# Memory attention with the query weights folded into the keys and the output weights into the values

## The chip, the cores and the metric

The kernel is one launch on one core of a Trainium2 chip. The core has a matrix engine (TensorE, "PE" in the profile, its weight loads "PEld"), a vector engine (VectorE, "DVE"), a scalar engine for activations (ScalarE, "ACT"), a general engine (GpSimd, "POOL") and a queue engine (SyncE, "SP"), which in this kernel issues all transfers. The metric is device time in microseconds of one execution; lower is better.

## The reference

One layer of an encoder, in fp32, for 2048 prompt tokens and 32 sample tokens (2080 columns), width 1024. Every sub-layer is `x + RMSNorm(sublayer(RMSNorm(x)))`:

1. token mixing: banded attention and gated linear attention from one input projection, joined by an output projection `w_o`;
2. attention with 4 heads of 256 into 256 memory tokens;
3. a SwiGLU feed-forward layer, hidden width 2816.

The change touches step 2 and its neighbours. Its core is

```
k = (m @ w_mk), v = (m @ w_mv)            # m = RMSNorm(mem), 256 x 1024, 4 heads of 256
q = h @ w_mq                              # h = RMSNorm(x)
p = softmax(q k^T / 16)                   # per head, over 256 memory tokens
out = concat_heads(p v) @ w_mo
```

The 32 sample tokens use keys and values from a cache instead of `k` and `v`. `k` and `v` of the prompt's memory are outputs too.

## The kernel before, in words

Activations lie feature-major: 128 features on the partitions, tokens along the free dimension. Nearly every fp32 product is made of three matmuls in a reduced-precision type (fp32r): each operand is split into a high part (a cast on ACT) and the remainder (a subtraction on DVE or POOL), and `mm3` (L485 in the profile) issues high x high, high x low, low x high into one PSUM bank. `mm3_steps` (L1329) is the same in pieces that can be interleaved with other work. `split` is L424/L425, `split_own` (in place) L429/L430. `load_w` and `w_piece` bring a weight tile of 128 x 512 from DRAM and split it.

The order of issue on each engine is not that of the program text. A class `Order` collects all operations, gives them costs and priorities, plans a schedule over all engines and then pins each engine to the planned order. So work of neighbouring stages is interleaved, and an engine never overtakes an instruction that it was given earlier. Where a pool of buffers closes and another opens over the same memory, the first users of the new tiles wait for the last users of the old.

The stages, in time: input projection and the two mixers, with the projections of the memory to keys and values (`mem_kv`) and the output projections of blocks 0 to 2 (`out_proj`, four blocks of 512, 512, 512, 544 tokens) interleaved, up to about 1250 us; the queries of the first 416 tokens (`mem_q0`, tile mqps at L1329) and the output projection of the last block (wops) up to about 1350; the memory stage up to about 1815; the feed-forward layer to the end.

The memory stage works on five blocks of 416 tokens (`CB`). `mem_q` projects the queries of the next block (mqps, L485; stored to DRAM, L1598); `mem_attn` loads them per head, makes scores (ms, sample tokens at L1635), softmax over rows of 104 or 128 tokens (L1637 to L1641), transposes (mpt, L1644) and the product with the values (mpv, sample tokens at L1654; mo, L1656/L1657). `mem_out` multiplies with `w_mo` (mops; copy to y at L1671). `mem_fin` applies the norm after the sub-layer, adds the residual and applies the norm ahead of the feed-forward layer (L1685 to L1690, `norm_fm` at L442 to L448), and stores x2d and h2d in DRAM in blocks of 416.

The feed-forward layer works on three blocks of two halves (`CF`: 348, 346, 346 tokens a half). Gate and up products (pg, pu) are computed by a scheme of seven instead of eight sub-products over the halves of tokens and features, the down product (pdn) accumulates into an SBUF tile acc (copy of the first product at L571, additions at L532). `finish` of a block makes the norm (n_ps L1876, rstd L434/L435), scales (L1883), adds the residual and stores `y_t` (L1886). Each block has new acc tiles, from a pool of two.

Of the kernel before, what the change touches and what calls it, by code (L numbers as in the profile page):

```python
# [393 lines left out]
def encoder_step(ctx, tc, ins, outs):  # L394
# [12 lines left out]
    QLEAD = 0.5  # L407
# [29 lines left out]

    def norm_fm(pool, pspool, xs, n, name, tag="dense", rbufs=2):
        acc = pool.tile([P, n], F32, tag="nacc", name=name + "_acc")
        for k in range(KT):  # L440
            if k == 0:
                ACT.activation(acc, xs[k], AF.Square)  # L442
            else:
                sq = pool.tile([P, n], F32, tag="nsq", name=f"{name}_sq{k}")
                ACT.activation(sq, xs[k], AF.Square)
                (POOL if k % 2 else DVE).tensor_tensor(out=acc, in0=acc, in1=sq, op=ALU.add)
        ps = pspool.tile([P, 512], F32, tag=tag, name=name + "_ps")
        PE.matmul(ps[:, :n], lhsT=ones, rhs=acc, start=True, stop=True)  # L448
        return rstd_of(pool, ps[:, :n], n, D, name + "_r", rbufs)

    def apply_split(pool, xs, g, r, n, dst, name):
        for k in range(KT):
            hf = pool.tile([P, n], F32, tag="hf", name=f"{name}_hf{k}")
            DVE.scalar_tensor_tensor(out=hf, in0=xs[k], scalar=g[:, k : k + 1], in1=r, op0=ALU.mult, op1=ALU.mult)
            hi, lo = dst[k]
            split(hi, lo, hf, POOL)
# [52 lines left out]
    mvd = dpool.tile([NMEM, D], F32, name="mvd")  # L509
    CB = [(i * 416, 416) for i in range(5)]  # L510
    h2d = [dpool.tile([D, n], F32, name=f"h2d{b}") for b, (_, n) in enumerate(CB)]
    x2d = [dpool.tile([D, n], F32, name=f"x2d{b}") for b, (_, n) in enumerate(CB)]
    qmd = [dpool.tile([D, n], F32, name=f"qmd{b}") for b, (_, n) in enumerate(CB)]
# [433 lines left out]
    with ExitStack() as ph:  # L947
# [448 lines left out]
        def mem_kv():  # L1396
            mv = []

            def first(tag):
                mv.clear()  # L1400
                for k2 in range(KT // 2):
                    m_ = mp.tile([P, 2, 544], F32R, tag="mov", name=f"mm{tag}_{k2}")
                    for j in range(2):
                        raw = sp.tile([P, 544], F32, tag="hr", name=f"mm{tag}_r{k2}_{j}")[:, :NMEM]
# [14 lines left out]
            def value(g4):  # L1419
                w = load_w(wp, ins["w_mv"][0], g4 * 256, 256, f"wmv{g4}")  # L1420
                for tt in range(2):
                    ps = pd.tile([P, 512], F32, tag="dense", name=f"mvps{g4}_{tt}")
                    yield from mm3_steps(ps[:, :256], [((mv[k][:, 0, tt * P : (tt + 1) * P], mv[k][:, 1, tt * P : (tt + 1) * P]), w[k]) for k in range(KT)], 12)
                    vf = sp.tile([P, 544], F32, tag="st", name=f"mvf{g4}_{tt}")[:, :256]
                    DVE.tensor_copy(vf, ps[:, :256])
                    SP.dma_start(mvd[tt * P : (tt + 1) * P, g4 * 256 : (g4 + 1) * 256], vf)
                    SP.dma_start(outs["mem_v"][0, 0].rearrange("t h d -> t (h d)")[tt * P : (tt + 1) * P, g4 * 256 : (g4 + 1) * 256], vf)
                    if tt == 0:
                        yield

            return [partial(first, 0)] + [partial(key, m) for m in range(KT)], [partial(first, 1)] + [partial(value, g) for g in range(4)]

        def mem_q0():
            n = CB[0][1]
            mv = {}

            def first():

                for k in range(KT):
                    pl, tag, w = [(lp, "ks", 768), (lp, "nb", 640), (gp, "W", 576), (xp, "xw", 544)][k // 2]  # L1440
                    kw = {"bufs": 2} if tag == "W" else {}
                    mv[k] = pl.tile([P, 2, w], F32R, tag=tag, name=f"hq0_{k}", **kw)
                    SP.dma_start(mv[k][:, 1, :n].bitcast(F32), h1d[0][k * P : (k + 1) * P, :n])
                    split_own(mv[k][:, :, :n], True)

            def query(m):
                w = load_w(wp, ins["w_mq"][0], m * P, P, f"wmq0_{m}")
                ps = (pd, pb, pb)[m % 3].tile([P, 512], F32, tag=("dense", "band", "band")[m % 3], name=f"mqps0_{m}")
                yield from mm3_steps(ps[:, :n], [(w[k], (mv[k][:, 0, :n], mv[k][:, 1, :n])) for k in range(KT)])
                qf = sp.tile([P, 544], F32, tag="hr", name=f"qf0_{m}")[:, :n]  # L1450
                ACT.mul(qf, ps[:, :n], 0.0625)
                SP.dma_start(qmd[0][m * P : (m + 1) * P, :], qf)

# [99 lines left out]
    with ExitStack() as ph:  # L1553
# [142 lines left out]
        for b in range(len(CB)):  # L1696
# [7 lines left out]
            if b != len(CB) - 2:  # L1704
                for it in proj:
                    it()
# [321 lines left out]
```

## Time and profile before

| | |
|---|---|
| median of 3 runs | 3280.02 us (3275.47 to 3282.64) |
| profiled execution: its span, the only time that is kept of it | 3277.0 us |
| instructions | 57899 |
| mean granted TensorE clock | 0.984 |
| busy: PE, DVE, ACT, POOL | 96%, 74%, 52%, 22% |
| transfers | 486.31 MB, mean 148 GB/s |

A span is the time from the first to the last instruction. Busy shares are averages over stages with different limits. In a view of groups, a line reads: code line, engine, operation, output<-inputs, partitions x elements, count | busy us, mean ns of one | idle time of the engine just before, with what ended it. In the chain (the work that ended last, followed back from the end) a row is start, length, engine, tile and count. In the waits a row is engine, tile and line, what it waited for, then total us, number of waits and the longest. Stretches are given in us from the span's start.

### The profile page before, as it was taken

How to read it: one execution, taken by the hardware profiler on the slowest of the kernel's cores; microseconds unless marked ns; L12 is line 12 of the kernel's file. 1: busy time of each engine (PE TensorE's matmuls, PEld its weight loads, DVE VectorE, ACT ScalarE, POOL GpSimd, SP SyncE). 2: the span in 40 equal slices, each digit the busy share in tenths (PEclk: the TensorE clock that was granted, in tenths of full speed). 3: DMA queues.
4: the chain of work that ended last, by engine and by line, in shares of the span. 5: the costliest groups of instructions: out<-in, count | busy, mean ns of one | idle time of the engine just before them, and what ended most of it. 6: DMA issues, size and time to landing. Idle time of an engine off the chain costs nothing.

```text
span 3277.0 us, 57899 instructions
## 1 busy us (share of the span) xinstructions
PE 3156.6 (96%) x21387; PEld 3022.0 (92%) x21387; DVE 2416.9 (74%) x4474; ACT 1719.9 (52%) x3706; POOL 717.1 (22%) x933
## 2 busy tenths in 40 slices
PE   7898999799999999999999899999899999899998
PEld 7888999698888888999999799999899999899998
DVE  7976976576575756777777877777977778977776
ACT  5645655656676666566665643334544334444344
POOL 0200100345474545410101111111211111311111
PEclk9999999899999999999999999999999999999999
DMA  5569273876585757765655522222432222422223
GB/s 150 178 168 297 101 222 120 262 227 193 177 269 152 239 169 229 221 191 179 204 175 179 166 91 71 76 78 78 136 111 78 76 73 63 130 79 77 78 78 96
DMA packets 490076, 486.31 MB, mean 148 GB/s; under 512 B 78528, under 2 KB 427881, under 8 KB 489793
## 3 DMA queue, kind: packets, MB, share of 16 engines
q1 hardware_dynamic: 489793, 482.61, 47.2%
q8 instruction: 168, 2.75, 0.3%
q14 instruction: 115, 0.94, 0.1%
HBM read 369.78 MB, written 113.83 MB: 148 GB/s over the span
## 4 chain that ended last, share of the span: by engine, by line
PE 88%; DVE 5%; DMA 3%; ACT 2%; issue 1%; SPq 1%; POOL 0%; DVEq 0%; ACTq 0%; POOLq 0%
PE pdn L485 15%; PE pg_X L485 8%; PE pu_X L485 7%; PE wops L1329 6%; PE mops L485 5%; PE mqps L485 4%; PE pg_Y L485 4%; PE pu_Y L485 4%; PE po L1063 4%; PE s L1058 2%; PE pg_Z L485 2%; PE pu_Z L485 2%; PE pt L1083 2%; PE ms L485 2%; PE g_s L1263 2%; PE wva_X L485 1%
## 5 line engine op out<-in xcount | busy, mean ns | idle before, releaser
L485 PE MATMUL pdn<-u,wd 128*128 128x346 f32 (+1 forms) x3168 | 520.2, 323 | 25.7 <-DVE acc L571 24.4
L485 PEld LDWEIGHTS pdn<-u,wd 128*128 128x128 f32 x3168 | 509.4, 190 | 27.7 <-DVE acc L571 25.3
L425 POOL TENSOR_TENSOR u<-sg,u 128x346 fp32r<-128x346 f32 (+1 forms) x132 | 165.4, 1264 | 1152.9 <-ACT u L424 611.7
L424 ACT CAST wg_s<-wg_r 128x512 fp32r<-128x512 f32 x231 | 139.1, 620 | 480.5 <-PE pdn L485 183.5
L532 DVE TENSOR_TENSOR acc<-acc,pdn 128x346 f32<-128x346 f32 (+1 forms) x464 | 235.8, 513 | 89.1 <-PE pdn L485 88.8
L485 PE MATMUL pg_X<-mf,wg_s 128*128 128x346 f32 (+1 forms) x1584 | 278.1, 324 | 6.6 <-ACT wg_s L424 5.3
L485 PE MATMUL pu_X<-mf,wu_s 128*128 128x346 f32 (+1 forms) x1584 | 275.2, 322 | 0.0
L485 PEld LDWEIGHTS pg_X<-mf,wg_s 128*128 128x128 f32 x1584 | 258.4, 190 | 8.2 <-ACT wg_s L424 5.7
L485 PEld LDWEIGHTS pu_X<-mf,wu_s 128*128 128x128 f32 x1584 | 256.9, 189 | 0.4
L1329 PE MATMUL wops<-om,wo_s 128*128 128x512 f32 (+1 forms) x960 | 214.4, 362 | 0.5 <-POOL om L430 0.5
L485 PE MATMUL mops<-mo,wmo_s 128*128 128x416 f32 x960 | 193.7, 353 | 2.1 <-DVE y L1671 1.2
L425 DVE TENSOR_TENSOR wu_s<-wu_r,wu_s 128x512 fp32r<-128x512 f32 x231 | 155.0, 696 | 39.1 <-ACT wu_s L424 39.0
L425 DVE TENSOR_TENSOR wd<-wd_r,wd 128x512 fp32r<-128x512 f32 x132 | 93.8, 715 | 121.7 <-ACT wd L424 121.6
L485 PEld LDWEIGHTS mops<-mo,wmo_s 128*128 128x128 f32 x960 | 177.1, 188 | 6.7 <-issue 1.9
L1329 PEld LDWEIGHTS wops<-om,wo_s 128*128 128x128 f32 x960 | 149.3, 188 | 20.5 <-issue 2.2
L485 PE MATMUL mqps<-m,wmq_s 128*128 128x416 f32 x768 | 163.6, 357 | 4.7 <-DVE m L430 4.2
L424 ACT CAST wu_s<-wu_r 128x512 fp32r<-128x512 f32 x231 | 136.6, 619 | 50.0 <-DVE wu_r L529 23.2
L425 DVE TENSOR_TENSOR wg_s<-wg_r,wg_s 128x512 fp32r<-128x512 f32 x231 | 158.7, 694 | 0.9 <-ACT wg_s L424 0.7
L1063 PE MATMUL po<-prt,v 128*128 128x128 f32 x1120 | 158.1, 281 | 1.2 <-PE mkps L1329 0.9
L1063 PEld LDWEIGHTS po<-prt,v 128*128 128x128 f32 x1120 | 145.3, 194 | 9.3 <-issue 2.9
L485 PE MATMUL pu_Y<-mf,wu_s 128*128 128x346 f32 (+1 forms) x792 | 140.1, 324 | 7.4 <-DVE up L532 5.7
L485 PEld LDWEIGHTS mqps<-m,wmq_s 128*128 128x128 f32 x768 | 139.8, 189 | 6.8 <-DVE m L430 4.4
(450 smaller groups left out, 7197.0 us busy)
## 6 DMA issues: line engine op xcount, KB each, us to landing
wg_r<-in_w_ffn_gate_dram SPq DMA_DIRECT2D x66, 512.0 KB, 4.4
wu_r<-in_w_ffn_up_dram SPq DMA_DIRECT2D x66, 512.0 KB, 3.5
wd_r<-in_w_ffn_down_dram SPq DMA_DIRECT2D x66, 512.0 KB, 3.4
wmq_r<-in_w_mq_dram SPq DMA_DIRECT2D x80, 256.0 KB, 3.0
wmo_r<-in_w_mo_dram SPq DMA_DIRECT2D x80, 256.0 KB, 3.0
q<-qd SPq DMA_DIRECT2D x32, 512.0 KB, 4.5
wo_r<-in_w_o_dram SPq DMA_DIRECT2D x64, 256.0 KB, 4.1
nb<-nbd SPq DMA_DIRECT2D x16, 640.0 KB, 7.6
```

What stands on the lines that cost most here:

```text
L424: ACT.copy(hi, src)
L425: (lo_eng or DVE).tensor_tensor(out=lo, in0=src, in1=hi.bitcast(F32), op=ALU.subtract)
L485: PE.matmul(ps, lhsT=a, rhs=b, start=first and i == 0, stop=last and i == len(seq) - 1, skip_group_check=skip)
L532: eng.tensor_tensor(out=out, in0=a, in1=b, op=ALU.add)
L1058: PE.matmul(ps_out, lhsT=q[:, 2 * i + e, q0 : q0 + nq], rhs=ks[:, e, k0 : k0 + ncol], start=i == 0, stop=i == 1)
L1063: PE.matmul(po[:, e * P : e * P + n], lhsT=v[:kk, j, e * 64 : e * 64 + P], rhs=prt[:kk, j, :n], start=j == 0, stop=j == len(rows) - 1)
L1083: PE.transpose(ptp[:kk, j, :n], pr[:n, c0 : c0 + kk], ident[:n, :n])
L1263: PE.matmul(sps[bk, li, :], lhsT=lh, rhs=rh, start=True, stop=True)
L1329: PE.matmul(ps, lhsT=a, rhs=b, start=i == 0, stop=i == len(seq) - 1)
```

## The change

The memory attention is computed in another association. Per head, `q k^T / 16 = h (Wq_h k_h^T / 16) = h G_h` with G_h of 1024 x 256, and `(p v_h) Wo_h = p (v_h Wo_h) = p H_h` with H_h of 256 x 1024.

- `mem_kv` projects the values transposed (as the keys) and normalises mem once; the values' output is transposed on the host.
- `mem_fold` takes the place of `mem_q0` ahead of the last output projection: it multiplies each head's keys with `w_mq` (handed over transposed by the host, `w_mq_t`) to gd[h], and its values with `w_mo` to hd[h], both in DRAM.
- The weight pool closes before the memory stage. That stage holds all four G in one tile gT, and works in 8 chunks of 256 tokens: scores of two heads at a time from h, 512 columns wide, softmax, transposes, and a store of the transposed probabilities to ptd. It no longer multiplies with values.
- The 32 sample tokens, whose keys and values are the cached ones, go the old way (queries, scores, values, output) in plain fp32, in pieces between the last chunks.
- The output product (probabilities with H) is made for the three feed-forward blocks in the buffers of the feed-forward stage (`mem_block`), with the norms and the residual per half block; x2d and h2d are stored by feed-forward block.
- In the feed-forward layer the two acc tiles are allocated once and serve all blocks, rstd stays in PSUM, `y_t` is stored in four pieces of two rows a half instead of two of four, and operand buffers are taken in another order.

The diff, cut to its core:

```diff
-    CB = [(i * 416, 416) for i in range(5)]
-    qmd = [dpool.tile([D, n], F32, name=f"qmd{b}") for b, (_, n) in enumerate(CB)]
+    mvd = dpool.tile([D, NMEM], F32, name="mvd")
+    gd = [dpool.tile([D, NMEM], F32, name=f"gd{h}") for h in range(HM)]
+    hd = [dpool.tile([NMEM, D], F32, name=f"hd{h}") for h in range(HM)]
+    QB = [(i * 256, 256) for i in range(TP // 256)]
+    ptd = [dpool.tile([D, n], F32, name=f"ptd{i}") for i, (_, n) in enumerate(QB)]
...
+            def keys_fold(h, a):
+                w = [w_piece(wp, ins["w_mq_t"][(2 * h + j) * P : (2 * h + j + 1) * P, a * 512 : a * 512 + 512].rearrange("p (k m) -> p k m", k=1), f"wqt{h}{a}{j}") for j in range(2)]
+                for i2 in range(2):
+                    ps = bank(2 * a + i2 + h, f"gps{h}{a}{i2}")
+                    for i in range(2):
...
+                        mm3(ps[:, i * NMEM : i * NMEM + NMEM], parts)
+                    gf = sp.tile([P, 544], F32, tag="hr", name=f"gf{h}{a}{i2}")[:, :512]
...
+                    SP.dma_start(gd[h][r0 : r0 + 256, :].rearrange("(i p) n -> p i n", p=P), gf.rearrange("p (i n) -> p i n", i=2))
...
+            def values_fold(h, a):
+                w = [w_piece(wp, ins["w_mo"][0][(2 * h + j) * P : (2 * h + j + 1) * P, a * 512 : a * 512 + 512].rearrange("p (k m) -> p k m", k=1), f"wov{h}{a}{j}") for j in range(2)]
+                for t in range(2):
+                    ps = bank(2 * a + t + h, f"hps{h}{a}{t}")
+                    mm3(ps, [...])
...
+                    SP.dma_start(hd[h][t * P : t * P + P, a * 512 : a * 512 + 512], hf)
...
-        for _ in steps(q0 + outp[3][0] + outp[3][1]):
+        for _ in steps(fold + outp[3][0] + outp[3][1]):
...
+    wph.close()
     with ExitStack() as ph:
...
+        gT = kp.tile([P, 2, KT, D], F32R, name="gT")
+        def load_g():
+            for h in range(HM):
+                v = gT[:, :, :, h * NMEM : h * NMEM + NMEM]
+                SP.dma_start(v[:, 1].bitcast(F32), gd[h].rearrange("(k p) n -> p k n", p=P))
+                for q in range(2):
+                    split_own(v[:, :, q * HK : q * HK + HK], q)
...
+        def token_tile(i, ht, pT, c):
+            cs = slice(c * P, c * P + P)
+            for hf in range(2):
+                ps = psc.tile([P, 512], F32, tag="sc", name=f"ms{i}_{c}_{hf}")
+                gs = slice(hf * 512, hf * 512 + 512)
+                mm3(ps, [((ht[:, 0, k, cs], ht[:, 1, k, cs]), (gT[:, 0, k, gs], gT[:, 1, k, gs])) for k in range(KT)])
...
+                softmax(pr, ps, P, st, 2)
...
+                ACT.copy(pT[:, hf * 4 : hf * 4 + 4, cs], pq)
...
+        def small_proj(src, mov, name):
...
+                    w = raw_w(src, m, q, f"{name}w{m}{q}")
+                    for k in range(HK):
+                        PE.matmul(ps[:, m], lhsT=w[:, k], rhs=mov[:, q * HK + k], start=q == 0 and k == 0, stop=q == 1 and k == HK - 1)
...
+        load_g()
+        own = sample()
+        for i in range(len(QB)):
+            chunk(i)
+            if i >= len(QB) - 3:
+                next(own, None)
...
-        pt = ph.enter_context(tc.tile_pool(name="cpt", bufs=1, space=PSUM, **RW))
-        pn = ph.enter_context(tc.tile_pool(name="cpn", bufs=1, space=PSUM, **RW))
+        pn = ph.enter_context(tc.tile_pool(name="cpn", bufs=2, space=PSUM, **RW))
+        pt = pn
+        accs = [xp.tile([P, KT, 348], F32, tag="acc", name=f"acc{ci}") for ci in range(2)]
...
+        def mem_block(b):
...
+                    for q, a0, a1, off in pieces(QB, s + c * n, s + c * n + nc_):
+                        SP.dma_start(lo[:, :, off : off + a1 - a0].bitcast(F32), ptd[q][kh * 512 : kh * 512 + 512, a0:a1].rearrange("(k p) n -> p k n", p=P))
+                    hi, lo = hi[:, :, :nc_], lo[:, :, :nc_]
+                    ACT.copy(hi, lo.bitcast(F32))
+                    DVE.tensor_tensor(out=lo, in0=lo.bitcast(F32), in1=hi.bitcast(F32), op=ALU.subtract)
+                    pq[kh, c] = (hi, lo)
...
+            def weights(g):
...
+                        for e in range(2):
+                            SP.dma_start(r[:, 2 * e : 2 * e + 2], hd[2 * kh + e][:, g * 256 : g * 256 + 256].rearrange("(k p) (a m) -> p k a m", p=P, a=2))
...
+            def unit_pair(g):
+                w = weights(g)
+                for a in range(2):
+                    m = 2 * g + a
+                    for c in range(2):
...
+                        mm3(ps[:, :nc_], [((w[kh, a][:, 0, k], w[kh, a][:, 1, k]), (pq[kh, c][0][:, k], pq[kh, c][1][:, k])) for kh in range(2) for k in range(HK)])
+                        (ACT.copy if c else DVE.tensor_copy)(ys_[c][m][:, :nc_], ps[:, :nc_])
+                        square(c, m)
...
+        for b in range(len(CF)):
+            us, fs = mem_block(b)
+            for i, it in enumerate(us):
+                it()
+                if i % 2 == 0 and fin:
+                    fin.pop(0)()
+            fin = fs
...
-            acc = [xp.tile([P, KT, 348], F32, tag="acc", name=f"acc{b}_{ci}") for ci in range(2)]
+            acc = accs
...
-                psn = pn.tile([P, 512], F32, tag="dense", name=f"n5_{b}_{ci}_ps")
-                PE.matmul(psn[:, :n], lhsT=ones, rhs=ssqs[ci], start=True, stop=True)
-                r = rstd_of(np_, psn[:, :n], n, D, f"n5_{b}_{ci}_r", 2, "nsq", 348)
+                r = pn.tile([P, 512], F32, tag="norm", name=f"n5_{b}_{ci}_ps")[:, :n]
+                PE.matmul(r, lhsT=ones, rhs=ssqs[ci], start=True, stop=True)
+                ACT.activation(r, r, AF.Ln, bias=eps_t, scale=1.0 / D)
+                ACT.activation(r, r, AF.Exp, scale=-0.5)
...
-                    c0 = s + ci * n - (TL if last else 0)
-                    SP.dma_start(outs["y_t"][kh * 512 : kh * 512 + 512, c0 : c0 + n].rearrange("(k p) n -> p k n", p=P), a[:, kh * HK : kh * HK + HK, :n])
+                        if kk % 2:
+                            c0 = s + ci * n - (TL if last else 0)
+                            SP.dma_start(outs["y_t"][(k - 1) * P : (k + 1) * P, c0 : c0 + n].rearrange("(k p) n -> p k n", p=P), a[:, k - 1 : k + 1, :n])
```

In this diff hd[h] and ptd are read per feed-forward block: tile wh holds a piece of hd, pq[kh, c] the probabilities of half c and heads 2 kh and 2 kh + 1. The function `finish` inside `mem_block` (not shown) makes rstd of the output product, loads x1 (x1r, one piece per row tile), scales, adds, stores x2d, and does the same again for h2d.

More of the change, by code (lines that the diff above doesn't have):

```diff
@@ L406, in encoder_step @@
     PRI = 4000
-    QLEAD = 0.5
     ident = cpool.tile([P, P], F32, name="ident")
@@ L436, in rstd_of @@
         return r
[L438 to L456, printed above, removed]
     def w_piece(wp, src, name, lo_eng=None):
@@ L1417, in key @@
                 SP.dma_start(outs["mk_t"][m * P : (m + 1) * P, :], kf[:, :NMEM])
[L1419 to L1428, printed above, removed]
-                        yield
@@ L1431, in mem_kv @@
[L1431 to L1452, printed above, removed]
-            return [first] + [partial(query, m) for m in range(KT)]
@@ L1803, in encoder_step @@
             ops = ffn_ops(0, ffn_raw(0))
+        for it in fin:
+            it()
         late = []
```

357 lines of the change are left out of this document (198 added, 159 removed).

## The prediction, before the run

> **What bounds the kernel now.** I read the page first (shares, transfers, chain), then busy time by stage, then TensorE's waits, then the chain in order of time, for the spacing of its matmuls.
>
> ```profile
> span 3277.0 us, 57899 instructions
> PE 3156.6 (96%) x21387; PEld 3022.0 (92%) x21387; DVE 2416.9 (74%) x4474; ACT 1719.9 (52%) x3706; POOL 717.1 (22%) x933
> ...
> q1 hardware_dynamic: 489793, 482.61, 47.2%
> HBM read 369.78 MB, written 113.83 MB: 148 GB/s over the span
> ...
> PE 88%; DVE 5%; DMA 3%; ACT 2%; issue 1%; SPq 1%; POOL 0%; DVEq 0%; ACTq 0%; POOLq 0%
> ```
>
> TensorE is the bound: 96% busy, 88% of the chain. So the change is worth the TensorE time that it removes, less the holes that it opens. 148 GB/s at a share of 47.2% is 315 GB/s for a full share; that is my transfer rate.
>
> ```profile
> 1249.00:1300.00 51.00, 50.79 (x315) 48.10 (x315) 28.46 (x50) 30.32 (x76) 28.29 (x27) 1.00 0.71 232
> 1300.00:1349.00 49.00, 49.00 (x392) 48.97 (x392) 26.12 (x40) 26.20 (x51) 11.49 (x8) 1.00 0.74 228
> 1349.00:1376.00 27.00, 22.84 (x129) 21.67 (x128) 25.72 (x30) 15.93 (x38) 19.63 (x12) 0.94 0.66 190
> 1376.00:1815.00 439.00, 436.19 (x2523) 420.71 (x2522) 336.75 (x646) 262.76 (x601) 55.73 (x45) 1.00 0.61 189
> 1815.00:1840.00 25.00, 18.38 (x97) 16.70 (x96) 24.64 (x31) 16.80 (x24) 2.15 (x2) 0.86 0.61 197
> 1840.00:1900.00 60.00, 51.33 (x291) 48.67 (x291) 50.16 (x84) 32.85 (x58) 9.83 (x8) 0.94 0.47 149
> 1900.00:3260.00 1360.00, 1334.83 (x8349) 1332.31 (x8348) 1034.30 (x1725) 573.99 (x1087) 201.67 (x164) 0.99 0.26 84
> ...
> 250.00:260.00 10.00, 5.40 (x20) 4.99 (x20) 6.21 (x10) 2.86 (x5) 0.00 (x0) 0.66 1.00 299
> 1280.00:1290.00 10.00, 10.00 (x55) 9.91 (x54) 3.52 (x7) 6.01 (x12) 3.53 (x3) 1.00 1.03 347
> 300.00:310.00 10.00, 10.00 (x54) 9.36 (x54) 5.78 (x14) 5.76 (x11) 0.00 (x0) 1.00 1.00 364
> ```
>
> Columns: stretch, its length, busy time (count) of PE, weight loads, DVE, ACT, POOL, then granted clock, transfer share, GB/s. 1249 to 1300 is the first block's memory queries, 1300 to 1349 the last output projection, up to 1815 the memory stage, then the feed-forward layer. At 1349 and 1815 TensorE has small holes; inside the stages none. The three rows with a share of 1.0 give 299 to 364 GB/s: the ends for my 315.
>
> ```profile
> PE pu_Y L485 <- DVE up L532: 5.7, 1, 5.7
> PE pg_X L485 <- ACT wg_s L424: 5.3, 1, 5.3
> PE mqps L485 <- DVE m L430: 4.2, 1, 4.2
> ...
> PE pdn L485 <- DVE acc L571: 24.4, 3, 11.9
> ```
>
> These are the only TensorE waits above 3 us after 1249; the largest falls where one feed-forward block gives way to the next.
>
> **TensorE work.** The chain gives the spacing of matmuls by moving width:
>
> ```profile
> 1137.14 1.88 PE wops L1329 x8
> ...
> 1270.64 29.52 PE mqps L1329 x156
> ...
> 1368.85 3.72 PE mqps L485 x11
> ...
> 1523.84 26.82 PE mops L485 x142
> ...
> 1647.77 1.40 PE ms L485 x12
> ...
> 1838.73 1.91 PE pu_X L485 x12
> ...
> 2359.29 15.28 DVE acc L1883 x14
> ...
> 2375.42 5.19 PE pdn L485 x22
> ...
> 2380.63 4.78 DMA out_dram<-acc
> ...
> 2854.03 12.50 PE pdn L485 x60
> ```
>
> 416 columns: 29.52/156 = 189 ns (mops the same). 512: 1.88/8 = 235. 256: 1.40/12 = 117. 348: 1.91/12 = 159. That is 0.46 ns a column throughout, so columns are what counts.
>
> ```profile
> L485 PE MATMUL mops<-mo,wmo_s 128*128 128x416 f32 x960 | 193.7, 353 | 2.1 <-DVE y L1671 1.2 <-DVE wmo_s L425 0.9
> ...
> L485 PE MATMUL mqps<-m,wmq_s 128*128 128x416 f32 x768 | 163.6, 357 | 4.7 <-DVE m L430 4.2 <-ACT qo L1598 0.6
> ...
> L485 PE MATMUL ms<-kTp,q 128*104 128x256 f32 (+1 forms) x456 | 73.0, 288 | 0.1
> ...
> L485 PE MATMUL mpv<-prR,vTp 128*128 128x416 f32 (+1 forms) x240 | 56.4, 352 | 0.0
> ...
> L1329 PE MATMUL mqps<-hq,wmq_s 128*128 128x416 f32 x192 | 38.2, 356 | 0.0
> ```
>
> Removed: queries 768+192 = 960 at 189 ns, 181.4 us; mops 960, 181.3; scores 456 at 117, 53.4; mpv 192 at 189 and 48 (384 wide) at 175, 44.7. Together 460.8 us.
>
> Added, counted from the code: folding queries into keys 4 heads x 8 row tiles x 2 x 3 = 192 at 117 ns, 22.5 us; values into output weights 96 at 235, 22.5; scores 16 token tiles x 2 halves x 24 = 768 at 235, 180.1; output product 3 blocks x 2 halves x 8 x 24 = 1152, 348, 346 and in one half 314 wide, 180.2. The 32 sample tokens stay unfolded in plain fp32: 2 x 64 products, 256 instructions, 32 columns wide:
>
> ```profile
> 1725.22 0.53 PE L1654 MATMUL mpv<-prT,vs 128*128 128x32 f32 x4
> 1725.58 0.36 PE L485 MATMUL ms<-kTp,q 128*128 128x256 f32 x1
> ```
>
> Four such start at 1725.22 and the next matmul at 1725.58: 90 ns each, 23.0 us. Together 428.3. The sample's own scores, the transposes and the norm products occur in both at about equal count. **Saving 32.5 us.** The value projection keeps its 192 matmuls; dropping the second normalisation of mem frees only ACT, DVE and SP, beside dense work, and I count nothing.
>
> **Old holes that go.** The windows' idle from 1349 to 1900 is 4.2 + 2.8 + 6.6 + 8.7 = 22.3 us. All of it belongs to work that is rebuilt: credited whole, what takes its place charged below.
>
> **Feed-forward block boundaries.** Now the first down products of a new block go through a copy into a new accumulator tile, which waits until every scale-and-add of the old one (DVE 15.28 us for 14, then POOL's adds) and its store (4.78 us) are over: 24.4 us. TensorE restarts slowly after a hole (11 matmuls of 416 columns in 3.72 us at 1368, where 2.1 would do): 22 matmuls in 5.19 us where 159 ns would give 3.5, 60 in 12.50 where they would give 9.5; 1.7 + 3.0 more, 29 us in all. After the change the accumulators persist, each pair of rows is stored by itself, the copy of row m waits only for its own pair, and the order puts the old block's norm product about 10 us earlier among TensorE's work. The store of a pair (4.78 us above) still lies in the way, in part behind other products, so I leave 3.5 us a boundary: **-22 us**. Ends: -29, and -5 if DVE's order still makes the copies wait for the whole scale chain.
>
> **New hole 1, the fold stage: +10 us.** A unit of 2.8 us (24 matmuls at 117 or 12 at 235) takes 0.52 MB of weights in and stores 0.52 MB. 16 units and the loads of K and V^T make 18.9 MB over 45 us of matmuls, 420 GB/s. About 2.6 MB can be prefetched or trail; the other 16.3 MB take 52 us at 315 GB/s, and SP's order costs something on top. Ends: 0 (45 us at 364) and 20. The stage that it replaces needed 232 GB/s.
>
> **New hole 2, between the last output projection and the first scores: +14 us.** The 64 KB-a-partition tile gT lies over the weight pool, closed one stage earlier now, so its loads wait for the last wops matmul, and nothing but two norm products is left for TensorE. The rows for a small load and for splitting 512 columns:
>
> ```profile
> wmq_r<-in_w_mq_dram SPq DMA_DIRECT2D x80, 256.0 KB, 3.0
> ...
> L424 ACT CAST wg_s<-wg_r 128x512 fp32r<-128x512 f32 x231 | 139.1, 620 | 480.5 <-PE pdn L485 183.5
> ...
> L425 DVE TENSOR_TENSOR wu_s<-wu_r,wu_s 128x512 fp32r<-128x512 f32 x231 | 155.0, 696 | 39.1 <-ACT wu_s L424 39.0
> ```
>
> Heads 0 and 1 (2.1 MB) take 6.7 us and about 2 to land (3.0 us for 256 KB, of which 0.8 is transfer), the ACT cast and the DVE remainder of 1024 columns twice 0.62 and 0.70, queues of DVE and POOL about 1: 12 idle, and 2 for the slow restart. In before, the next queries' operands lay ready, and 4.2 us were lost. Ends 7 and 20.
>
> **New hole 3, between scores and output product: +25 us.** pq000 waits for the last score matmul (its tile lies on the score operands). SP then issues in order: 3 sample weight pieces, hd pieces, the last chunk's store, pq001, more hd, pq100 to pq111 for the next block, pq011, five x1r, and only then pq010, which itself waits for the last sample matmul. The order on TensorE puts one matmul of mo0_0_1 (reads pq010) ahead of all of mo0_1_0 (data ready long before), so everything stands behind it. 10.6 MB at 315 GB/s are 34 us; TensorE has some 10 us of sample products, transposes and mo0_0_0 to fill it. 24 idle, with the restart 25. Ends 14 (most of the queue overtaken or landed) and 34.
> By the Trainium skill, "DMA: Bandwidth & Descriptors", section Bandwidth, a large transfer reaches 425 GB/s; the 10.6 MB would take an estimated 25 us and the hole be 15, the sum 10 us lower. The trace has no stretch above 364, so I stay with 315.
>
> **The output product and the feed-forward start: +11 us.** Per block: 4.2 MB of hd (read three times in all), and 2.85 MB each of pq, x1r, x2d, h2d: 15.6 MB in 60 us, 260 GB/s, under 315 but with heads of SP's queue waiting for buffers: 5 us. The first gate products wait for the cast of h2d operands as now (5.3 + 5.7), with more lead: 6 us. Ends 3 and 25. Per block DVE and ACT have some 80 operations of 0.5 to 0.7 us each there, under the 60 us; the softmax of a tile half is some ten operations of that size or smaller on both, beside 5.6 us of TensorE. The sample's 8 MB of raw weights need 27 us beside 67 us of score work. If that cover went, each us would be a us.
>
> **Sum** against the profiled span: -32.5 - 22.3 - 22 + 10 + 14 + 25 + 11 = -16.8, so 3260.2. The median of the runs, 3280.0, lies 3.0 above the span (their own spread is 7): 3263.
>
> **Rivals.**
> *Slower: the output product is starved.* 47 MB pass one in-order queue in 180 us of matmuls. I charged 5 us; at a rate R the stage lasts 47/R. The gain of 17 is gone at 180 + 5 + 17 = 202 us, 233 GB/s. At 220 GB/s it is 214 us, +12: 3292. For it: the 1249 to 1349 rows move 228 to 232 GB/s at shares of 0.71 to 0.74, the best this queue holds over 50 us in company of matmuls there. Against: the share shows that it was not asked for more. 20%.
> *Boundaries keep their wait.* DVE's order alone decides; -5 in place of -22: 3280, no change. 12%.
> *Holes mostly filled.* Fold 0, hole 2 at 9, hole 3 at 14, the rest 5, boundaries -25: -52, 3228. For it: 300 to 310 shows 364 GB/s with TensorE full. 15%.
> *The clock falls through the fold stage.* At 250 to 260 TensorE was 54% busy beside a full queue and the granted clock 0.66; at 0.7 the fold's 45 us become 64 in place of 55: +9, 3272. 1349 to 1376, 85% busy, kept 0.94. 5%.
> By the Trainium skill, "TensorE: Matmul & The Clock Gate", section HAM oscillation, waits above about 3.4 us between short bursts bring the clock to half each time; the 250 row agrees, and the fold, with waits near 1 us a unit, would escape by that rule.
> That the work is not saved at all is hardly a case: spacing goes by columns in every row above.
>
> **Chances.** The sum's case has 48%, its own range 3250 to 3276. What a measurement can tell from no change is 0.2%, 6.6 us: 3273.5 to 3286.6. Faster: the sum's case 44, filled holes 15, clock 3, boundaries 3: 65%. Same: 4 of the sum's case, 9 of the boundaries, 2 of the clock, 1 of the first rival: 16%. Slower: the other 19 of that rival. Range 3226 to 3298.
>
> **What would show it.** Right: 960-count mqps and mops groups gone, ms 768 and mo 1152 at the spacings above; TensorE idle of some 12 us ahead of the first ms, waiting for gT, and 20 or more ahead of the second mo group, waiting for pq; pdn's wait for acc down to about 7; the fold at 300 GB/s with TensorE near 82% busy. Wrong: pdn's wait still 20; the output product's stretch well over 190 us with waits for wh or pq; a hole at the start of gates above 10; or changes ahead of 1249, where the same work is only ordered anew.

## The result, and the profile after

The changed kernel takes 3316.26 us (median of 4 runs, 3309.29 to 3320.66) against 3279.58 for the kernel before in the same runs: a ratio of 1.011, 95% interval 1.0095 to 1.0124. It is slower by 37 us where I had forecast 17 us faster, and it lies outside my range (3226 to 3298). The profiled execution is the slowest of the four, 3320.66 us with a span of 3318.9.

From the page of the changed kernel, lines as in the first fence of the prediction:

```profile
span 3318.9 us, 56688 instructions
PE 3150.5 (95%) x21215; PEld 2979.3 (90%) x21215; DVE 2279.9 (69%) x4153; ACT 1629.0 (49%) x3471; POOL 791.0 (24%) x993
```

TensorE's busy time fell by only 6 us; its time without work rose by 48. Part of the shorter work is hidden in that busy time, because a matmul counts as busy for longer where the granted clock falls: of the fold's hps matmuls the middle one was recorded with 396 ns and the longest with 797.

Five points that both traces have, by the start of the matmul in question, tell where the time went (us from the span's start; the stretch between two points in brackets):

| point | before | changed | difference of the stretch |
|---|---|---|---|
| first memory query / first matmul of the fold | 1250.8 | 1259.7 | +8.9 |
| last matmul of the last output projection | 1347.8 (97.0) | 1402.4 (142.7) | +45.7 |
| first memory scores of the stage behind it | 1348.7 (0.9) | 1413.6 (11.2) | +10.3 |
| first down product of the feed-forward layer | 1884.5 (535.8) | 1954.5 (540.9) | +5.1 |
| last matmul | 3270.0 (1385.5) | 3311.6 (1357.1) | -28.4 |

The feed-forward layer gained what I had forecast and a little more. The fold stage lost 46 us, and the memory stage with the output product, which has 41 us less to multiply (32.5 in all, and 8.7 that the fold has more than the queries it replaces), came out no shorter.

Busy time by stretch of the changed kernel, columns as before (stretch, length, PE, weight loads, DVE, ACT, POOL, granted clock, transfer share, GB/s):

```profile
1275.00:1300.00 25.00, 17.14 (x118) 15.22 (x116) 19.91 (x30) 12.10 (x30) 9.99 (x7) 0.93 0.89 282
1300.00:1325.00 25.00, 11.20 (x55) 9.38 (x56) 10.11 (x13) 13.65 (x20) 11.73 (x8) 0.78 0.95 330
1325.00:1350.00 25.00, 17.79 (x60) 12.27 (x59) 9.81 (x15) 8.34 (x14) 1.07 (x1) 0.87 0.78 242
...
1375.00:1400.00 25.00, 25.00 (x202) 25.00 (x202) 5.91 (x10) 7.66 (x15) 5.92 (x5) 1.00 0.11 33
1400.00:1425.00 25.00, 11.38 (x44) 8.30 (x44) 15.78 (x8) 11.88 (x16) 16.24 (x7) 0.66 0.67 213
...
1650.00:1675.00 25.00, 12.24 (x51) 11.89 (x50) 9.54 (x11) 10.50 (x14) 0.00 (x0) 0.50 1.05 322
1675.00:1700.00 25.00, 19.19 (x107) 18.90 (x107) 12.04 (x13) 9.69 (x14) 1.99 (x2) 0.84 0.56 183
...
1875.00:1900.00 25.00, 11.72 (x50) 9.41 (x49) 23.89 (x27) 12.44 (x19) 16.36 (x12) 0.61 0.84 258
1900.00:1925.00 25.00, 16.93 (x91) 16.17 (x90) 23.43 (x36) 14.04 (x28) 14.00 (x13) 0.80 0.82 261
```

The reader sees four holes: the fold (1260 to 1356) with the queue nearly full, followed by an output projection during which the queue stands at 33 GB/s; the start of the scores at 1400; the start of the output product at 1650, with the queue full; and the start of the feed-forward layer at 1875, with the queue not full but DVE at 24 of 25 us. TensorE's waits that belong to them:

```profile
PE mo L464 <- ACT wh L423: 12.8, 1, 12.8
PE hps L464 <- DVE hf L1453: 12.6, 5, 6.8
PE gps L464 <- DVE gf L1441: 10.8, 4, 6.1
...
PE pg_Y L464 <- ACT mf L423: 8.2, 1, 8.2
PE pg_X L464 <- DVE sg L516: 8.1, 1, 8.1
...
PE mo L464 <- ACT pq L1785: 5.8, 1, 5.8
PE ms L464 <- ACT gT L428: 5.6, 1, 5.6
...
PE ms L464 <- DVE gT L429: 4.8, 1, 4.8
PE pdn L464 <- DVE acc L555: 4.0, 3, 2.2
```

The wait of pdn for acc, 24.4 us before, is 4.0.

### The profile page after: what moved, and what is told of

The parts are those of the page before. It is cut to its first block, busy times and chain, and to the rows that moved or that the text cites. A ratio compares the mean times of both kernels' runs of the same rounds, so it can differ in the third digit from the quotient of the medians.

```text
span 3318.9 us, 56688 instructions
## 1 busy us (share of the span) xinstructions
PE 3150.5 (95%) x21215; PEld 2979.3 (90%) x21215; DVE 2279.9 (69%) x4153; ACT 1629.0 (49%) x3471; POOL 791.0 (24%) x993
## 4 chain that ended last, share of the span: by engine, by line
PE 86%; DMA 4%; DVE 4%; issue 2%; ACT 2%; SPq 1%; POOL 1%; DVEq 0%; POOLq 0%; ACTq 0%
PE pdn L464 15%; PE pg_X L464 7%; PE pu_X L464 7%; PE wops L1313 6%; PE ms L464 5%; PE mo L464 4%; PE pg_Y L464 4%; PE po L1047 4%; PE pu_Y L464 4%; PE s L1042 2%; PE pg_Z L464 2%; PE pt L1067 2%; PE pu_Z L464 2%; PE g_s L1247 2%; PE wva_X L464 1%
## 5 line engine op out<-in xcount | busy, mean ns | idle before, releaser
L464 PE MATMUL ms<-gT,hm 128*128 128x512 f32 x768 | 193.5, 403 | 10.3 <-ACT gT L428 5.6
L464 PE MATMUL mo<-pq,wh 128*128 128x346 f32 (+2 forms) x1056 | 174.1, 326 | 18.6 <-ACT wh L423 12.8
L464 PEld LDWEIGHTS mo<-pq,wh 128*128 128x128 f32 x1056 | 170.3, 193 | 20.5 <-ACT wh L423 12.9
L464 PEld LDWEIGHTS ms<-gT,hm 128*128 128x128 f32 x768 | 143.5, 192 | 40.7 <-ACT gT L428 6.4
L464 PE MATMUL pg_Y<-mf,wg_s 128*128 128x346 f32 (+1 forms) x792 | 137.6, 322 | 8.2 <-ACT mf L423 8.2
```

Of the source, the lines that this page charges most:

```text
L464: PE.matmul(ps, lhsT=a, rhs=b, start=first and i == 0, stop=last and i == len(seq) - 1, skip_group_check=skip)
```

## The experiments

All times are medians, and ratios are to the kernel before in the same runs. A new order is planned for each kernel, and that alone moves the beginning: the fold starts between 1248 and 1262 us in the profiles of its variants. So I read stretches in the profiles first and whole times second.

### Four result tiles for the fold

The fold's results (gf, hf) lie in the tag hr of a pool of two. A unit's copy out of PSUM therefore waits until the store before last has landed.

```diff
-                    gf = sp.tile([P, 544], F32, tag="hr", name=f"gf{h}{a}{i2}")[:, :512]
+                    gf = sp.tile([P, 544], F32, tag="st" if i2 else "hr", name=f"gf{h}{a}{i2}")[:, :512]
...
-                    hf = sp.tile([P, 544], F32, tag="hr", name=f"hf{h}{a}{t}")[:, :512]
+                    hf = sp.tile([P, 544], F32, tag="st" if t else "hr", name=f"hf{h}{a}{t}")[:, :512]
```

> The changed kernel with the fold's result tiles spread over two tags (every second one under tag st in place of hr), so four tiles in place of two wait for their stores. Theory 'two buffers' (each fold unit waits until the store before last has landed, 4.0 us by the median): the stretch from the first gps to the first wops of the last output projection shrinks from some 90 us to 60 to 65, the waits of gps and hps for gf and hf (26 us now) to under 6, time 3285 to 3292. Theory 'transfers' (26.3 MB through one queue at 277 GB/s in that stretch): at 330 GB/s the same bytes still take 80 us, so at most 10 us go; time 3306 to 3316, and the waits move from gf and hf to the weight pieces.

Measured: 3301.52 us, ratio 1.0063 (1.0046 to 1.0079). The stretch from the first gps to the last hps went from 96.3 to 83.0 us; time and stretch lie between the two forecasts. Windows of this stretch, the changed kernel and then the variant:

```profile
1259.70:1356.00 96.30, 67.07 (x371) 55.87 (x371) 53.95 (x81) 46.85 (x94) 37.22 (x29) 0.88 0.84 274
```

```profile
1248.00:1331.00 83.00, 68.08 (x393) 53.58 (x393) 57.03 (x82) 46.81 (x96) 39.22 (x32) 0.94 0.94 315
```

The waits for gf and hf are gone but for some 3 us, and others took their place:

```profile
PE hps L464 <- ACT wov_s L423: 8.1, 6, 3.9
...
PE hps L464 <- DVE wov_s L424: 2.7, 5, 1.1
```

So both hold, one behind the other: the two tiles cost up to 13 us, and behind them stands the queue, with a share of 0.94. 26.1 MB in 83 us are 315 GB/s, just the rate that I had taken; it was the bytes that I had wrong. The largest groups of transfers issued in the changed kernel's stretch (count, KB each, us to landing):

```profile
gd<-gf SPq DMA_DIRECT2D x16, 256.0 KB, 4.0
wov_r<-in_w_mo_dram SPq DMA_DIRECT2D x16, 256.0 KB, 4.9
hd<-hf SPq DMA_DIRECT2D x14, 256.0 KB, 2.7
om<-od SPq DMA_DIRECT2D x8, 272.0 KB, 5.2
wqt_r<-in_w_mq_t_dram SPq DMA_DIRECT2D x8, 256.0 KB, 3.3
h1d<-y SPq DMA_DIRECT2D x8, 256.0 KB, 3.7
hm<-h1d SPq DMA_DIRECT2D x2, 1024.0 KB, 7.6
wo_r<-in_w_o_dram SPq DMA_DIRECT2D x6, 256.0 KB, 3.1
sqw<-in_w_mq_dram SPq DMA_DIRECT2D x5, 256.0 KB, 4.8
...
```

om, h1d, hm, wo and sqw, nine to ten MB, are not the fold's: they are the end of one stage and the lead of two others.

### Half of the weight pieces

To see whether transfers bind what is left, this kernel has the four tiles and loads each second weight piece only; both splits are made from the same raw tile, and half of the weights is left out of the result.

```diff
+    def w_twin(wp, src, name):
...
+            raw = wp.tile([P, 512], F32, tag="wraw", name=name + "_r")
+            SP.dma_start(raw, src)
+            res = []
+            for j in range(2):
+                w = wp.tile([P, 2, 512], F32R, tag="wsp", name=f"{name}{j}_s")
+                split(w[:, 0], w[:, 1], raw)
+                res.append((w[:, 0:1], w[:, 1:2]))
...
+                w = w_twin(wp, ins["w_mq_t"][2 * h * P : (2 * h + 1) * P, a * 512 : a * 512 + 512], f"wqt{h}{a}")
...
```

> The fold with four result tiles (3301.5 us), with only every other weight piece of w_mq_t and w_mo loaded and split twice into two tiles, so that ACT, DVE and TensorE do the same work and 4.2 of some 26.5 MB are not moved (half of the weights is left out of the result). Theory that transfers bind what is left of the fold (share 0.93 there): the stretch from the first gps to the last hps goes from 83 us to 70 to 73, time 3288 to 3293. Rival, that casts and waits for TensorE's own results bind it: 80 us or more, time 3298 to 3304.

Measured: 3293.38 us, ratio 1.0033 (1.0019 to 1.0047). The stretch is 77.1 us, 6 less for 4.2 MB less, in the middle between the forecasts. The waits for wov are gone, but there is one new wait of 8.3 us:

```profile
PE hps L476 <- ACT hf L1465: 8.3, 1, 8.3
```

The copy that ended this wait stood on ACT behind casts of hm, an operand of the next stage, and for hm's load ACT itself waited (in the timeline a row is start, length, instruction, and in brackets the idle time before it):

```profile
1308.79 1.99 ACT L428 CAST hm<-hm 128x1024 fp32r<-128x1024 f32 x2 [2.84 <-DMA hm<-h1d]
1311.48 1.05 ACT L428 CAST hm<-hm 128x1024 fp32r<-128x1024 f32 x1 [0.70 <-DMA hm<-h1d]
1312.43 0.58 ACT L1465 COPY hf<-hps 128x512 f32<-128x512 f32 x1
```

Without this wait the stretch would be 69, which would speak for transfers; with it the run settles nothing by itself. What it does show is a third limit beside tiles and bytes: the planned order can put a copy that TensorE waits for behind the next stage's work on the same engine. In the changed kernel the longest wait for hf, 6.8 us, also ends with a copy that DVE makes right behind a remainder of hm (at 1323.77, behind 1322.62), so not all of the 13 us above need be the tiles'.

### The fold put alternately with the last output projection

```diff
-        for _ in steps(fold + outp[3][0] + outp[3][1]):
+        for _ in steps(weave(fold, outp[3][0] + outp[3][1])):
```

> The changed kernel with the fold's 17 units put alternately with the row tiles of the last output projection instead of ahead of them. Both theories expect a gain, of different size. 'Two buffers': units come 5 to 6 us apart, more than a store's landing, so no wait for gf or hf is left: fold and projection together take 96 to 100 us in place of 142, time 3272 to 3280. 'Transfers': some 31 MB at 280 GB/s take 110 us, time 3284 to 3292. If neither holds and the slow clock of the stretch is what costs, it is the gap in counts of matmuls that closes: time 3290 to 3300.

Measured: 3290.07 us (10 runs), ratio 1.0026 (1.0014 to 1.0037), 26 us less than the changed kernel. From the first gps to the last wops it takes 113.2 us where it was 142.7, and the last hps now starts 2.6 us behind that:

```profile
1256.80:1370.00 113.20, 104.43 (x723) 95.97 (x722) 66.56 (x98) 60.12 (x121) 40.16 (x29) 0.97 0.75 250
```

TensorE is 92% busy, at a clock of 0.97, and the queue's share is 0.75. The time is the one forecast for 'transfers' (110 us; 3284 to 3292), but not for its reason: at a share of 0.75 the queue does not bind, and of the waits for gf and hf only 1.1 us are left, as 'two buffers' had it. So the number was hit by luck, and the run does not decide between the two. What it shows is that the same work and bytes, spread over a stage that needs few transfers, are mostly hidden.

### The buffers of the output product

```diff
-        MORD = (4, 5, 6, 0, 1, 2, 3)
-        PORD = ((0, 1, 2, 3), (4, 5, 6), (0, 1, 2, 3))
+        MORD = (4, 2, 3, 0, 1, 5, 6)
+        PORD = ((0, 1, 5, 6), (4, 2, 3), (0, 1, 5, 6))
```

> The changed kernel with the operand buffers of the first feed-forward block's second half taken from tiles that come free with the last score matmul (numbers 5 and 6 in place of 2 and 3, which wait for the sample's last product). My account of the hole between scores and output product: the second wait of mo (5.8 us for pq) goes, the first (12.8 us) stays or shrinks; -5 to -10, time 3306 to 3311. Rival, that the hole is only the 10.6 MB that must pass in any order: no change, 3314 to 3319.

Measured: 3308.02 us, ratio 1.0086 (1.0066 to 1.0105). The wait for pq is gone, and the stretch from the first to the last mo went from 195.6 to 186.5 us. The first wait stays, the only one of mo that is left:

```profile
PE mo L464 <- ACT wh L423: 13.6, 1, 13.6
```

So the hole has the two parts that I had named together: one matmul placed ahead of work that was ready (9 us with the slow restart, and it goes), and the first operands behind a full queue (13 us, and it stays).

### The second finish of each block earlier

```diff
-                if i % 2 == 0 and fin:
+                if fin:
```

> The changed kernel with the second half's norms and residual of each block issued behind the second quarter of the next block's output product in place of the third. Theory: the feed-forward layer's first operands (hr) lie in the stage tiles that block 1's second half (y1 1) holds until its last h2d store, so they come late because that finish is late: pg's waits for mf (8.2 and 2.6 us) go, the layer's first down product comes 8 to 14 us earlier, time 3302 to 3309. Rival, that DVE (24 of 25 us busy from 1875 to 1900) is the bound there: the waits move to other tiles, time 3313 to 3319.

Measured: 3304.81 us, ratio 1.0077 (1.0062 to 1.0092). By the time this would be a hit, by the profile it is a miss: from the first mo to the first pdn the two kernels take 284.3 and 284.7 us. The 11 us lie elsewhere (the fold starts 7.7 us earlier and the scores take 4 us less, some 3 of them because the granted clock, which falls to half among them in the changed kernel, did not fall there), where the edit has no part. pg's waits did move rather than go:

```profile
PE pg_X L464 <- DVE sg L516: 8.0, 1, 8.0
...
PE pg_Y L464 <- ACT mf L423: 5.3, 1, 5.3
PE n L1833 <- POOL ms L516: 5.3, 1, 5.3
...
PE pg_X L464 <- ACT mf L423: 3.5, 1, 3.5
```

### Less for DVE at the start of the feed-forward layer

The first scaling of the last block's finish is left out, and with it that part of the result.

```diff
-                    DVE.scalar_tensor_tensor(out=y[m], in0=y[m], scalar=gains["g_post_mem"][:, m : m + 1], in1=r, op0=ALU.mult, op1=ALU.mult)
+                    if b < len(CF) - 1:
+                        DVE.scalar_tensor_tensor(out=y[m], in0=y[m], scalar=gains["g_post_mem"][:, m : m + 1], in1=r, op0=ALU.mult, op1=ALU.mult)
```

> The changed kernel without the first scaling (16 DVE operations of some 0.5 us) in the finish of the last block of the output product; that part of the result is left out. Theory that DVE, 23 to 24 of each 25 us busy from 1875 to 1925, is the bound at the start of the feed-forward layer: the stretch from the last mo to the first pdn, 89.1 us in the changed kernel, shrinks to 79 to 83, time 3306 to 3311. Rival, that it is the loads behind SP's order (h2d stores of block 1 ahead of the first hr) that bind: 88 to 90 us, and the time stays at 3314 to 3319.

Measured: 3305.45 us, ratio 1.007 (1.0055 to 1.0085). From the last mo to the first pdn it takes 79.6 us where the changed kernel took 89.1. Sixteen of the DVE operations of the changed kernel's group below, at 568 ns, are 9.1 us: what DVE is spared comes off the time. So its work is on the path there, and the rows of 1875 and 1900, where it has hardly any idle time, say the same. The scalings are also a link in the finish that the next layer waits for; whether any other 9 us of DVE's work would be worth as much was not tried. The group, then the stretch in the changed kernel and in this one:

```profile
L1845 DVE SCALAR_TENSOR_TENSOR acc<-acc,g_post_mem,n 128x348 f32<-128x348 f32 (+1 forms) x32 | 16.5, 568 | 0.6 <-ACT n L1835 0.6
```

```profile
1865.40:1954.50 89.10, 62.90 (x350) 59.24 (x349) 81.06 (x116) 51.12 (x94) 42.84 (x36) 0.83 0.70 217
```

```profile
1861.10:1940.70 79.60, 60.08 (x337) 55.63 (x336) 70.67 (x88) 48.13 (x89) 40.73 (x33) 0.85 0.70 219
```

### Accumulators and stores undone

```diff
-            acc = accs
+            acc = [xp.tile([P, KT, 348], F32, tag="acc", name=f"acc{b}_{ci}") for ci in range(2)]
...
-                        if kk % 2:
-                            c0 = s + ci * n - (TL if last else 0)
-                            SP.dma_start(outs["y_t"][(k - 1) * P : (k + 1) * P, c0 : c0 + n].rearrange("(k p) n -> p k n", p=P), a[:, k - 1 : k + 1, :n])
+                    c0 = s + ci * n - (TL if last else 0)
+                    SP.dma_start(outs["y_t"][kh * 512 : kh * 512 + 512, c0 : c0 + n].rearrange("(k p) n -> p k n", p=P), a[:, kh * HK : kh * HK + HK, :n])
```

> The changed kernel with new accumulator tiles for each feed-forward block and y_t stored in two pieces a half, as before. If the persistent accumulators with the finer stores are what shortens the wait at the two block boundaries (24.4 us before, 4.0 after): the wait of pdn for acc is back above 18 us, time 3332 to 3340. Rival, that the order planned anew did it: wait under 8 us, time 3313 to 3320.

Measured: 3319.63 us, ratio 1.012 (1.0103 to 1.0137). That is 3 us above the changed kernel, which the scatter of the runs does not tell from nothing; as a time it is the rival's. The wait of pdn for acc is 10.5, between the two forecasts:

```profile
PE pdn L464 <- DVE acc L555: 10.5, 2, 5.4
```

From the first down product to the last matmul this kernel takes 1360.5 us, the changed one 1357.1 and the kernel before 1385.5. Most of the gain at the boundaries, then, comes from something else in the change.

### The kernel before with the accumulators alone, and with the PSUM tiles too

The same two edits, made in the kernel before:

> The kernel before with nothing but the accumulators kept over the blocks and y_t stored in four pieces a half. If these two by themselves shorten the boundary waits (24.4 us) as I wrote: 3258 to 3264. By the undo in the changed kernel, where they were worth about 3 us in time and 6.5 in pdn's wait: 3272 to 3278. If they help only where the norm product has been moved ahead: 3280 to 3283.

Measured: 3272.25 us (10 runs), ratio 0.9972 (0.9962 to 0.9981). Then with the norm's PSUM pool of two and rstd left in PSUM:

```diff
-        pt = ph.enter_context(tc.tile_pool(name="cpt", bufs=1, space=PSUM, **RW))
-        pn = ph.enter_context(tc.tile_pool(name="cpn", bufs=1, space=PSUM, **RW))
+        pn = ph.enter_context(tc.tile_pool(name="cpn", bufs=2, space=PSUM, **RW))
+        pt = pn
...
-                psn = pn.tile([P, 512], F32, tag="dense", name=f"n5_{b}_{ci}_ps")
-                PE.matmul(psn[:, :n], lhsT=ones, rhs=ssqs[ci], start=True, stop=True)
-                r = rstd_of(np_, psn[:, :n], n, D, f"n5_{b}_{ci}_r", 2, "nsq", 348)
+                r = pn.tile([P, 512], F32, tag="norm", name=f"n5_{b}_{ci}_ps")[:, :n]
+                PE.matmul(r, lhsT=ones, rhs=ssqs[ci], start=True, stop=True)
+                ACT.activation(r, r, AF.Ln, bias=eps_t, scale=1.0 / D)
+                ACT.activation(r, r, AF.Exp, scale=-0.5)
...
```

> The kernel before with all of the change's feed-forward part that bears on the block boundary: kept accumulators, y_t in four pieces a half, and rstd left in a PSUM tile of a pool of two (in place of one tile there and a copy in SBUF). Kept accumulators and finer stores alone brought pdn's wait for acc from 24.4 to 13.7 us and the time to 3272. If the second PSUM tile is what lets the norm product of the second half go ahead, and so is the rest of what the changed kernel shows (wait 4.0): wait 3 to 6 us, time 3259 to 3266. If the rest comes from the changed kernel's order of operands and loads: wait 11 to 14, time 3270 to 3275.

Measured: 3261.21 us (5 runs), ratio 0.9935 (0.9922 to 0.9947): the fastest kernel here, 55 us under the changed one. The wait for acc in the one and in the other:

```profile
PE pdn L485 <- DVE acc L571: 13.7, 3, 6.6
```

```profile
PE pdn L485 <- DVE acc L571: 3.2, 3, 1.5
```

24.4 us with neither edit, 13.7 with the accumulators alone, 10.5 with the PSUM part in the changed kernel without the accumulators, 3.2 and 4.0 with both. From the first down product to the last matmul the kernel before takes 1373.5 us with the accumulators alone (12.0 less than before) and 1362.3 with both (11.2 less again), so in the kernel before the two are of about equal weight. The changed kernel's 1357.1 are another 5 us less, which no run explains, and there the accumulators are worth 3.4 only: the parts overlap. What the PSUM part does in detail (the second tile, or the copy to SBUF that is saved) was not taken apart.

### All four repairs of the memory part together

The four tiles, the alternation, the buffers and the earlier finish in one kernel:

> The changed kernel with the four result tiles, the fold put alternately with the last output projection, the exchanged operand buffers and the earlier second finish, all in one. If the four effects hit different waits they add up: -26 for the mixing with at most 3 more for the tiles, -8 for the buffers, -8 to -12 for the finish; 3270 to 3278, a little under the kernel before. If the transfers that are moved out of the fold only come up elsewhere: 3285 to 3292.

Measured: 3282.36 us (10 runs), ratio 1.0003 (0.9992 to 1.0014): no different from the kernel before. By their sizes alternation and buffers add up (26 + 8 of the 34 us gained), and the tiles and the finish give nothing on top; which edit gave what inside this kernel was not taken apart. It has the feed-forward part of the change too, so with its folded attention it still stands 21 us behind the kernel that took that part alone.

## Why the prediction was wrong, point by point

- **TensorE work, -32.5.** The counts are right (ms 768, mo 1152), and the spacings nearly: 82 scores in 18.63 us are 227 ns where I had 235, 456 of mo in 74.50 are 163 where I had 159. The step that failed is the 90 ns of the sample's small matmuls, read off four in a row: the 256 of them take 31 us, not 23. These rows of the chain are spacings of 227, 137 and 163 ns:

```profile
1472.01 18.63 PE ms L464 x82
...
1563.74 5.48 PE sq L1632 x40
...
1682.58 74.50 PE mo L464 x456
```

  Those of the small matmuls are not at one clock: 211 of the 256 start at the full granted clock and stand 104 ns apart, 43 at half of it and stand 210 apart (the last section shows where). So some 4 us of the 8 are the spacing and some 4 the clock. The gain is about 24 to 28 us.
- **Old holes, -22.3, and what takes their place.** They went, and new ones of the same kind came. My "ahead of 1249 the same work is only ordered anew" cost 8.9 us in this profile, a wait for a table (fl) that grew from 2.5 to 5.9 us among it; over the variants the fold's start lies between 1248 and 1262, so this is scatter of the planner more than the change.
- **The fold, +10: the term that failed.** It cost +37 beyond its matmuls (45.7 in the stretch, less 8.7 of work). The step is "18.9 MB over 45 us": it counted the transfers of the moved step and not those that other stages put into the same queue in that time, and it did not ask in which tiles the results wait for their stores. 26.3 MB at my 315 GB/s give 83.5 us, and the variant with four tiles took 83.0. I had 420 GB/s on the paper and made 10 us of it by letting 2.6 MB come early or trail and putting the other 16.3 MB at 52 us; nothing trails in the row of 1375, 33 GB/s, because the order keeps the light stage behind the heavy one. The waits for the two tiles were in the sum at nothing but "something on top".
- **Hole 2, +14.** 11.2 us up to the first score, then another wait of 4.8 us and a slow restart (clock 0.66 in the row of 1400), some 18 in all: the place and the wait for gT are right, the size 4 us short.
- **Hole 3, +25.** TensorE waits 12.8 us ahead of the first mo and 5.8 inside it, 18.6 where I had 24; the clock in the rows of 1650 and 1675, 0.50 and 0.84, costs some 5 more where I had 1. That is 23 in all: the place is right, and the exchanged buffers show its inner part, but more slow clock made up for a shorter wait. That clock was at half before the hole began, beside the sample's last matmuls (last section). The queue moved 322 GB/s at a share of 1.05 from 1650 to 1675, near my 315. In that stretch the 425 GB/s of the Trainium skill's page "DMA: Bandwidth & Descriptors", section Bandwidth, weren't reached. The hole, 23, came out nearer the 25 of my rate than the 15 that I had worked out from that figure. My reason for staying with 315 was misread, though: the kernel before has stretches above 364, 382 GB/s from 910 to 920.
- **Output product and feed-forward start, +11.** The waits of pg and n there come to some 27 us with the clock at 0.61 and 0.80. The step that failed is "under the 60 us": I weighed DVE against a whole block and not against the 89 us in which the last block's finish, the first operands' splits and the first gate weights all fall on it. Leaving out 9 us of its work took 9.5 us off. My rival of the starved queue was not it: from 1700 to 1850 the windows show mo without a hole, at 73 to 262 GB/s.
- **Block boundaries, -22.** -28.4 in the stretch. The size was nearly right, the cause only in part: in the kernel before, kept accumulators and finer stores are 12.0 of it and the second PSUM tile with rstd in place 11.2, and some 5 stay unexplained. The prediction counted on an earlier norm product, but gave the PSUM part no share of the gain.
- **The fall of the clock through the fold**, my 5% rival: 0.93, 0.78, 0.87 in the rows of 1275 to 1350. It fell, but with the four tiles TensorE waited for data at 0.94 all the same, so it is not what makes the stage long; that it follows the waits is my reading of it. My estimate of waits near 1 us was wrong: they reach 6.8 us. The rule of the Trainium skill's "TensorE: Matmul & The Clock Gate", section HAM oscillation, agrees with the waits of up to 6.8 us here.

Of the miss of 59 us in the profiled span (3318.9 where I had 3260.2), the fold is 27, the start of the feed-forward layer 16 to 20, the beginning 9, the sample 8 and hole 2 4; the boundaries gave 6 back and hole 3 2.

## What to carry to other kernels

A step that moves from one stage to another brings its bytes into a queue that others use: list every transfer that is issued in that stretch, not only the step's own, and look at what the stage next to it moves; putting a heavy and a light stage alternately was worth 26 us for one line. Ask of each new result in which tile it waits for its store, and how many of them there are. And when one change has several parts, make the small ones alone: here the part that was an aside is the one to keep, 0.65% faster on its own, while the kernel that has the idea of the change as well is 21 us slower than that part alone, even with the four repairs.

## What was not expected of the hardware

The granted clock fell while TensorE had no idle time. These rows are from the changed kernel, where the sample's 32-column matmuls run beside the scores: the first two cover 40 of them in a row, the third the scores behind, the fourth a stretch where they come in eights between scores, the last the end of the sample:

```profile
1563.60:1566.70 3.10, 3.10 (x31) 3.10 (x29) 2.19 (x5) 1.98 (x6) 0.33 (x1) 1.00 0.69 192
1566.80:1569.00 2.20, 2.20 (x12) 2.20 (x12) 0.00 (x0) 0.00 (x0) 0.00 (x0) 0.50 1.11 360
1569.00:1573.60 4.60, 4.60 (x14) 3.62 (x14) 0.00 (x0) 0.00 (x0) 0.00 (x0) 0.50 0.68 203
1576.30:1582.75 6.45, 6.45 (x51) 6.07 (x49) 1.92 (x5) 1.15 (x5) 2.40 (x1) 1.00 0.80 242
1648.70:1656.80 8.10, 8.10 (x41) 8.10 (x40) 1.61 (x1) 1.94 (x2) 0.00 (x0) 0.50 1.01 312
```

Some 3 us into the run of 40 the clock goes to half, with TensorE 100% busy, and the scores behind it start at half the clock as well; in eights between scores it stays at 1.00. At the last 24 and 32 in a row it falls again, ahead of the hole at the output product. In all nine profiles with this code it falls at that last run, and in seven of them during or right behind the run of 40. Why it falls there was not tested.

The queue's rate was not the same throughout. In the kernel with four result tiles, the half of the fold that loads and stores pieces of H ran faster than the half with G, whose results go out in rows half as long (256 elements in place of 512):

```profile
1248.00:1286.80 38.80, 37.23 (x297) 33.35 (x298) 35.94 (x54) 24.52 (x60) 23.21 (x22) 1.00 0.85 264
1290.00:1320.00 30.00, 18.11 (x55) 11.86 (x56) 14.95 (x18) 16.23 (x26) 16.00 (x10) 0.88 1.07 386
```

386 GB/s over 30 us is above the 364 that I had taken for the upper end. Per unit of share that is 361 against 311. That the row length is the reason was not tested; the second stretch also has two loads of 1 MB (hm).
